# A hybrid decoder block on one core: the order of the first loads, dummy matmuls up to the first product, and a new order of the mixer's products

## The chip, the cores and the metric

The kernel runs on one core of a Trainium2 chip. TensorE (PE) multiplies, VectorE (DVE) and ScalarE (ACT) work element by element, GpSimd (POOL) and SyncE (SP) mostly issue transfers here. The metric is the device time of one execution in microseconds (us). Lower is better.

## The reference

One layer of a decoder trunk over 16 meta tokens and 256 tokens, width 2048, in float32:

```python
u = rms_norm(h, g_pre_mix[l])
proj = u @ w_in[l]
z_pool, v_conv, g_conv, gate_a, gate_b = jnp.split(proj, splits, axis=-1)
y_a = causal_multiscale_pool(z_pool, w_pool_grp[l], pool_scale[l]) @ w_pool_out[l]
y_b = conformer_conv(v_conv, g_conv, w_dw[l], b_dw[l],
                     conv_ln_g[l], conv_ln_b[l]) @ w_conv_out[l]
m = jax.nn.sigmoid(gate_a) * y_a + jax.nn.sigmoid(gate_b) * y_b
h = h + rms_norm(m @ w_o[l], g_post_mix[l])
u = rms_norm(h, g_pre_mlp[l])
f = jnp.square(jax.nn.relu(u @ w_up[l])) @ w_down[l]
h = h + rms_norm(f, g_post_mlp[l])
```

The convolution has 31 taps per channel and is followed by a LayerNorm and a swish. The output is the 256 tokens without the meta tokens.

## The kernel before

**Numbers.** Every float32 operand is split in a rounded high part (a copy on ACT, `hi`) and the rest (a subtraction on DVE, `lo`), and a product is three matmuls: high by high, high by low, low by high. The weights come in blocks of 1 MB (128 partitions by 2048 floats), each loaded by a DMA that SP issues, split by one ACT copy and one DVE subtraction, and read by PE. Three split blocks are held at a time.

**Start.** SP and ACT issue the first loads: the meta tokens, the gain row `g_pre_mix`, the tokens `x` in four blocks of 512 columns (the first in two halves of 128 tokens, `load_x` and the lines around it), and the first two weight chunks in small pieces (`open_chunk`, L335). POOL issues five rows of vectors and the taps (`load_rows`, L396, L425). PE runs dummy transposes of an identity (`keep_warm`, L434), turns the gain row into a column (L403), then the meta tokens (`meta_tiles`, L482) and the token tiles (`x_tile`, L472). ACT and DVE scale and split them into `u` (L474, L475, L490, L491). Then a loop over the 16 row tiles k turns token tile k + 3, splits weight piece k + 3 (`pieces_to`) and multiplies tile k (`mm3`, L515).

**Mixer.** What follows is planned when the kernel is built. `Plan.add` takes work with an engine, a cost and names read and written; `Plan.order` simulates the engines: PE's order is fixed by the program, the others take the ready work with the earliest due time, and transfers share the DMA by `ISSUE` (issue and start-up time of a queue) and `LANDS`. The result fixes the instruction order of every engine; the real waits are semaphores. PE's order is the table `MAIN`, one word a step. First letter: p is the projection of the pooling branch, a and b are the two gates, c the convolution's projection, o the output projection. A word with two digits, such as a13, is two plain products (both halves of 128 tokens) of column block 1 and row block 3. A word with P, such as a0P5, is one of seven products that stand for eight (Strassen's scheme) on column blocks 0 and 1: P5, P6, P4 and P7 need the sum of two weight blocks. The sum is made on DVE where the table `SUMMED` names it (L805); elsewhere POOL issues a DMA that adds the second block onto the first while it lands (L809, "bring"). T31 turns column block 3 of the second token half of the merged branches for the output projection (L1303; low part L1312). `fu`, `OF` and `um8` make the combined activations ("forms") that the P-products read; `lnm` and `lnv` are the matmuls for the LayerNorm's mean and variance (L1042, L1072), after which half 0 and half 1 of its result (`s_act`, L1100) are made; `CD`, `h1`, `k0r`, `k1` open rooms. While PE multiplies, DVE also does the 240 taps of the convolution (L923).

**MLP.** A second plan of the same kind, from about 510 us to the end (L520, L526, L1921).

## Time and profile before

| | us |
|---|---|
| median of 3 runs | 1193.89 |
| lowest, highest | 1192.64, 1197.27 |
| the profiled execution | 1195.48 |
| its span | 1193.4 |

The profile is of one execution. Idle time of an engine is put down to what ended it. A row of the timeline is a start, a length in us, the engine, the line, the operation, the names written and read, and the count. Names lose their numbers in the profile, so bank_k is any of four PSUM banks and acc_v either of two.

### The profile page before, as it was taken

What the parts mean: (1) busy time and instruction counts of PE and PEld (TensorE: products, weight loads), DVE (VectorE), ACT (ScalarE), POOL (GpSimd) and SP (SyncE); (2) the same over time, 40 slices, a digit from 0 to 9 for tenths busy, and PEclk for the clock granted to TensorE, in tenths of its full rate; (3) what the DMA queues carried; (4) which work ended last, traced back from release to release, by engine and by line L of the source; (5) the groups of instructions that cost most, each with busy time, mean ns of one, the idle gap of its engine ahead of it and who ended that gap; (6) DMA issues with size and microseconds to landing.
All of it is one profiled execution on the core that took longest, in us unless ns stands there. A gap on an engine that the chain in (4) does not pass through costs nothing.

```text
span 1193.4 us, 15768 instructions
## 1 busy us (share of the span) xinstructions
PE 1171.5 (98%) x6318; PEld 1012.9 (85%) x6318; DVE 1079.1 (90%) x1162; ACT 711.5 (60%) x718; POOL 53.3 (4%) x54
## 2 busy tenths in 40 slices
PE   9999999999999999999999999999999999999996
PEld 8999988777878777898888888888888888888885
DVE  6799999999998988687989989989999999899856
ACT  7634354565478746557776666666656756666542
POOL 1000000000000000000100000000000000000000
PEclk9999999999999999999999999999999999999998
DMA  9756353878767779549998897998998998979931
GB/s 314 249 183 218 107 173 109 282 199 285 203 198 253 247 229 316 177 128 359 230 343 222 244 317 179 261 310 191 297 279 213 306 236 233 316 184 264 329 140 71
DMA packets 181481, 280.23 MB, mean 235 GB/s; under 512 B 4657, under 2 KB 92145, under 8 KB 180496
## 3 DMA queue, kind: packets, MB, share of 16 engines
q1 hardware_dynamic: 160224, 235.35, 58.1%
q0 software_dynamic: 20160, 42.10, 19.9%
q10 hardware_dynamic: 1024, 1.78, 0.4%
q8 instruction: 49, 0.80, 0.3%
q14 instruction: 24, 0.20, 0.0%
HBM read 275.02 MB, written 4.19 MB: 234 GB/s over the span
## 4 chain that ended last, share of the span: by engine, by line
PE 76%; DVE 14%; DMA 4%; issue 3%; ACT 2%; DVEq 0%; POOL 0%; ACTq 0%; POOLq 0%
PE bank_u L520 18%; PE acc_up L1921 13%; PE bank_u L526 9%; PE bank_a L1921 7%; PE bank_k L1199 7%; DVE lo L793 6%; PE bank_k L515 6%; PE bank_b L1921 5%; DMA raw_p<-in_w_in_dram 3%; PE acc_v L515 3%; DVE c L923 3%; PE acc_v L1199 3%; PE acc_up L520 1%; ACT hi L788 1%; DVE raw_p L805 1%
## 5 line engine op out<-in xcount | busy, mean ns | idle before, releaser
L520 PE MATMUL bank_u<-m,hi 128*128 128x512 f32 x960 | 329.4, 390 | 0.0
L526 PE MATMUL bank_u<-m,lo 128*128 128x256 f32 x960 | 265.3, 276 | 0.0
L520 PEld LDWEIGHTS bank_u<-m,hi 128*128 128x128 f32 x960 | 180.2, 188 | 37.8
L788 ACT CAST hi<-raw_p 128x2048 fp32r<-128x2048 f32 x70 | 134.1, 1915 | 114.5 <-PE bank_k L1199 34.3
L526 PEld LDWEIGHTS bank_u<-m,lo 128*128 128x128 f32 x960 | 180.2, 188 | 1.6
L1747 DVE TENSOR_TENSOR lo<-raw_m,hi 128x2048 fp32r<-128x2048 f32 x71 | 162.5, 2289 | 15.2 <-ACT hi L1742 14.9
L793 DVE TENSOR_TENSOR lo<-raw_p,hi 128x2048 fp32r<-128x2048 f32 x70 | 160.0, 2290 | 16.9 <-ACT hi L788 16.7
L1742 ACT CAST hi<-raw_m 128x2048 fp32r<-128x2048 f32 x71 | 136.0, 1916 | 51.4 <-PE bank_u L520 18.0
L1921 PE MATMUL acc_up<-hi,forms 128*128 128x512 f32 x440 | 143.0, 390 | 0.7 <-ACT G L1946 0.7
L1742 ACT CAST hi<-raw_h 128x2048 fp32r<-128x2048 f32 x46 | 88.1, 1915 | 50.2 <-PE bank_u L520 32.5
L1747 DVE TENSOR_TENSOR lo<-raw_h,hi 128x2048 fp32r<-128x2048 f32 x46 | 105.3, 2290 | 12.8 <-ACT hi L1742 12.7
L923 DVE SCALAR_TENSOR_TENSOR c<-a,taps,c 128x256 f32<-128x256 f32 x240 | 100.5, 485 | 0.0
L1921 PEld LDWEIGHTS acc_up<-hi,forms 128*128 128x128 f32 x440 | 82.6, 188 | 18.8 <-ACT G L1946 1.1
L515 PE MATMUL bank_k<-u_um,hi 128*128 128x272 f32 x512 | 95.2, 287 | 0.0
L1199 PE MATMUL bank_k<-hi,u_um 128*128 128x512 f32 x272 | 86.8, 391 | 1.8 <-DVE sg L1244 1.1
L1921 PE MATMUL acc_up<-lo,forms 128*128 128x512 f32 x220 | 85.9, 391 | 0.0
L1921 PE MATMUL bank_a<-hi,forms 128*128 128x512 f32 (+1 forms) x256 | 82.0, 383 | 0.0
L515 PEld LDWEIGHTS bank_k<-u_um,hi 128*128 128x128 f32 x512 | 79.7, 188 | 0.0
L515 PE MATMUL bank_k<-u_um,lo 128*128 128x272 f32 x256 | 73.3, 287 | 0.0
L1742 ACT CAST hi<-raw_a 128x2048 fp32r<-128x2048 f32 x23 | 44.0, 1914 | 34.0 <-PE bank_u L520 25.0
L1921 PE MATMUL bank_b<-hi,forms 128*128 128x512 f32 (+1 forms) x200 | 63.4, 381 | 0.0
L1747 DVE TENSOR_TENSOR lo<-raw_a,hi 128x2048 fp32r<-128x2048 f32 x23 | 52.7, 2291 | 11.3 <-ACT hi L1742 11.3
(392 smaller groups left out, 2248.1 us busy)
## 6 DMA issues: line engine op xcount, KB each, us to landing
raw_p<-in_w_in_dram SPq DMA_DIRECT2D x34, 1024.0 KB, 5.8
raw_m<-in_w_up_dram SPq DMA_DIRECT2D x25, 1024.0 KB, 9.8
raw_m<-in_w_down_dram SPq DMA_DIRECT2D x22, 1024.0 KB, 8.5
raw_h<-in_w_down_dram SPq DMA_DIRECT2D x21, 1024.0 KB, 7.6
raw_h<-in_w_up_dram SPq DMA_DIRECT2D x16, 1024.0 KB, 8.7
raw_a<-in_w_down_dram SPq DMA_DIRECT2D x12, 1024.0 KB, 5.6
raw_a<-in_w_up_dram SPq DMA_DIRECT2D x11, 1024.0 KB, 7.0
raw_m<-in_w_down_dram POOLq DMA_DIRECT2D x11, 1024.0 KB, 9.2
```

What stands on the lines that cost most here:

```text
L515: nc.tensor.matmul(acc, w[:, k[0], cs], act[:, k[1], a, off:], start=first and n == 0, stop=last and n == 2)
L520: nc.tensor.matmul(acc.rearrange("p (a t) -> p a t", a=2)[:, :, ts], hi[:, k[0], cs], act[:, k[1], :, off + ts.start:off + ts.stop], start ...
L526: nc.tensor.matmul(acc[:, :T], lo[:, k[0], cs], act[:, k[1], 0, off:], start=False, stop=stop, skip_group_check=True)
L788: nc.scalar.copy(box["flat"], rooms[q]())
L793: nc.vector.tensor_sub(lo, rooms[q](), f32(box["flat"]))
L805: plan.add("DVE", 2.22, lambda a=at_rooms[0], b=at_rooms[1]: nc.vector.tensor_add(rooms[a](), rooms[a](), rooms[b]()), reads=names, writes ...
L923: nc.vector.scalar_tensor_tensor(C_c()[:, q, :], A_a()[:, q, i:i + T], taps[:, q, i:i + 1], C_c()[:, q, :], op0=ALU.mult, op1=ALU.add)
L1199: nc.tensor.matmul(banks[bank], a_(k, part), box[w_][:, k, :], start=opens and k == 0 and i == 0, stop=ends_ and k == CK - 1 and i == 2, s ...
L1742: nc.scalar.copy(box["flat"], raw_in(room))
L1747: nc.vector.tensor_sub(lo, raw_in(room), f32(box["flat"]))
L1921: nc.tensor.matmul(acc, forms[h][:, f, k, a_, :], box[w_][:, k, cs], start=start and k == 0 and n == 0, stop=stop and k == KH - 1 and n == ...
```

## The change

1. The first loads are issued in another order: the two halves of token block 0 first (one on ACT's queue, one on SP's), then the meta tokens (SP) and the gain row (ACT), then the weight pieces with token blocks 1, 2 and 3 between them on SP (`X_BEHIND`). The five vector rows and the taps go from POOL's queue to SP's, behind the third weight chunk.
2. The meta tokens' split is cut in four parts: the first behind token tile 0, the others in the first three turns of the loop. The loop multiplies tile k before it turns tile k + 3.
3. Of 14 + 4 dummies, 13 stay ahead of the gain's transpose, and 5 stand between the third token tile and the first product.
4. The planner's constants change (`ISSUE`, `LANDS`, `SHARE`, costs of transfers): while both queues move data, POOL's gets 3.55 times the share of SP's.
5. `MAIN` is a new order of the same 96 steps, and `SUMMED` makes 9 instead of 11 sums on DVE: a0P5, a2P6, c2P5 and o0P5 become DMA additions, a2P7 and o0P4 become sums.

```diff
-DUMMIES = 4
+DUMMIES = (13, 5)
@@
 MAIN = (
-    "p00 p01 fu p11 p10 p20 p30 p21 p31 k1 a0P1 a0P5 a13 a0P6 a12 a0P7 a03 a0P3 a2P1 a0P4 a2P5 "
-    "a02 a33 a2P6 a2P3 a2P2 a2P7 a23 a32 a0P2 b0P1 a22 a2P4 b0P5 b32 b23 b33 b21 b22 lnm b0P6 b20 "
-    "b0P7 lnv b03 b12 b0P2 b13 b0P4 b0P3 k0r b30 b31 b02 um8 c01 c2P1 c2P5 c00 c2P6 c2P3 c2P7 "
-    "c2P2 c2P4 T00 T01 c10 CD T31 T30 o0P1 c11 T20 o23 T11 T10 o20 o21 T21 OF o22 o0P5 o0P6 o0P3 "
-    "o0P7 o12 o0P2 o03 o0P4 o13 h1 o02 o30 o31 o32 o33 ")
-SUMMED = {('gate0', 0): '567', ('gate0', 2): '56', ('gate1', 0): '5', ('co', 2): '564', ('o', 0): '56'}
+    "p00 p01 p30 p31 p21 p20 fu p10 p11 k1 a0P1 a0P2 a2P1 a0P5 a13 a12 a0P6 a0P3 a0P7 a02 a0P4 "
+    "a2P5 a2P2 a32 a03 a2P6 a2P3 a33 a2P7 a22 a23 a2P4 b33 b32 b20 b0P1 b31 b0P5 b23 b22 b0P6 "
+    "b0P3 lnm b0P7 b30 b21 lnv b12 b0P2 b0P4 b02 b13 b03 k0r um8 c2P1 c00 c11 c01 T00 c2P5 c2P6 "
+    "c2P3 c10 T01 c2P7 T10 o20 c2P2 T11 c2P4 o0P1 CD T30 T31 o21 T20 T21 o23 OF o0P2 o0P5 o22 o13 "
+    "o0P6 o0P3 o0P7 o12 o0P4 h1 o03 o02 o30 o31 o32 o33 ")
+SUMMED = {('gate0', 0): '67', ('gate0', 2): '57', ('gate1', 0): '5', ('co', 2): '46', ('o', 0): '46'}
@@ class Plan
-    ISSUE = {"SP": (0.4, 1.0), "POOL": (1.28, 2.2)}
-    LANDS = 1.0
+    ISSUE = {"SP": (0.4, 1.09), "POOL": (1.28, 2.44)}
+    LANDS = 1.13
+    SHARE = {"SP": 1.0, "POOL": 3.55}
@@ def open_chunk
             nc.sync.dma_start(raw[:, sl, :], src[:, sl, :])
+            if (n, b_) in X_BEHIND:
+                load_x(X_BEHIND[n, b_])
@@
-    nc.sync.dma_start(m_in, meta)
-    pre_rows = load_rows(nc.scalar, "g_pre_mix")
-    for t, queue in enumerate((nc.scalar, nc.sync)):
-        queue.dma_start(x_in[:, t, :CW], xv[:, t, :CW])
-    load_x(nc.scalar, 1)
-    for b in range(2, XB):
-        open_chunk()
-        load_x(nc.sync, b)
-    open_chunk()
-    other_rows = load_rows(nc.gpsimd, "pool_scale", "b_dw", "conv_ln_g", "conv_ln_b", "g_pre_mlp")
+    X_BEHIND = {(0, 4): 1, (0, 8): 2, (1, 4): 3}
+    for t, queue in enumerate((nc.scalar, nc.sync)):
+        queue.dma_start(x_in[:, t, :CW], xv[:, t, :CW])
+    nc.sync.dma_start(m_in, meta)
+    pre_rows = load_rows(nc.scalar, "g_pre_mix")
+    for _ in range(FIRST + 1):
+        open_chunk()
     taps_in = big.tile([TAPS, CC], F32, tag="c", name="taps_in")
-    nc.gpsimd.dma_start(taps_in, w_dw)
+    nc.sync.dma_start(taps_in, w_dw)
+    other_rows = load_rows(nc.sync, "pool_scale", "b_dw", "conv_ln_g", "conv_ln_b", "g_pre_mlp")
@@
-    keep_warm(14)
+    keep_warm(DUMMIES[0])
     rows_to_columns(*pre_rows)
-    keep_warm(DUMMIES)
@@
-    for k in range(-LEAD, KD):
-        if k + LEAD < KD:
-            x_tile(k + LEAD)
-        pieces_to(k + LEAD + 1)
-        if k < 0:
-            continue
+    def turn_and_split(k):
+        if k < KD:
+            x_tile(k)
+        if k == 0:
+            meta_parts.pop(0)()
+        pieces_to(k + 1)
+
+    for k in range(LEAD):
+        turn_and_split(k)
+    keep_warm(DUMMIES[1])
+    for k in range(KD):
+        for j, acc in enumerate(accs):
+            mm3(acc, *opened[k // HALF[0]][:2], u, (k % HALF[0], k), slice(j * P, (j + 1) * P),
+                k == 0, k == KD - 1)
+        turn_and_split(k + LEAD)
+        if k < 3:
+            meta_parts.pop(0)()
...
-        for j, acc in enumerate(accs):
-            mm3(acc, *opened[k // HALF[0]][:2], u, (k % HALF[0], k), slice(j * P, (j + 1) * P),
-                k == 0, k == KD - 1)
```

In the planner a moving transfer advances by its queue's share of the sum of shares instead of by an equal part, and its cost falls from 3.1 or 2.9 to 3.06 or 2.87 on SP, from 5.9 to 4.94 for an addition on POOL.

How PE's rows move at the start (idle is the dummies' bank, pv the gain's transpose, mt_in the meta tokens', xt a token tile's, acc_v the first product). Before:

```order
L434 MATMUL idle<-ident 128x128 x14
L403 MATMUL pv_g_pre_mix<-ident,rows_g_pre_mix 128x16
L434 MATMUL idle<-ident 128x128 x4
L482 MATMUL mt_in<-ident,m_in 128x16 x16
L472 MATMUL xt_185<-ident,x_in 128x128 x2
L472 MATMUL xt_192<-ident,x_in 128x128 x2
L472 MATMUL xt_199<-ident,x_in 128x128 x2
L472 MATMUL xt_206<-ident,x_in 128x128 x2
L515 MATMUL acc_v_0_183<-u_um,hi_83 128x272 x2
```

The same place in the change (its own line numbers):

```order
L436 MATMUL idle<-ident 128x128 x13
L407 MATMUL pv_g_pre_mix<-ident,rows_g_pre_mix 128x16
L483 MATMUL mt_in<-ident,m_in 128x16 x16
L473 MATMUL xt_172<-ident,x_in 128x128 x2
L473 MATMUL xt_181<-ident,x_in 128x128 x2
L473 MATMUL xt_188<-ident,x_in 128x128 x2
L436 MATMUL idle<-ident 128x128 x5
L519 MATMUL acc_v_0_170<-u_um,hi_83 128x272 x2
```

The four dummies behind the gain's transpose are gone, five stand ahead of the first product, and the fourth token tile comes behind it.

POOL's row of block additions in the mixer (w_in holds the gates; raw_p, raw_k, raw_um, raw_s0b are rooms). Before:

```order
L809 DMA raw_p_417<-in_w_in_dram 128x4x512
L809 DMA raw_p_415<-in_w_in_dram 128x4x512
L809 DMA raw_k_2237<-in_w_in_dram 128x4x512
L809 DMA raw_p_417<-in_w_in_dram 128x4x512
L809 DMA raw_p_415<-in_w_in_dram 128x4x512 x2
L809 DMA raw_p_416<-in_w_conv_out_dram 128x4x512
```

In the change:

```order
L822 DMA raw_p_415<-in_w_in_dram 128x4x512 x2
L822 DMA raw_p_417<-in_w_in_dram 128x4x512 x2
L822 DMA raw_p_416<-in_w_in_dram 128x4x512
L822 DMA raw_p_417<-in_w_in_dram 128x4x512 x2
L822 DMA raw_p_416<-in_w_conv_out_dram 128x4x512
L822 DMA raw_p_415<-in_w_conv_out_dram 128x4x512
```

Seven blocks of the gates and two of the convolution's projection are added by DMA, instead of six and one; two of the output projection stay.

DVE around T21, where m is the low part of a turned block, q_m and forms_o serve the output projection's P-products. Before:

```order
L805 TENSOR_TENSOR raw_p_416<-raw_p_416,raw_um_3358 128x2048
L1169 TENSOR_TENSOR sg_2259<-acc_v_0_183,sg_2259 128x512
L1312 TENSOR_TENSOR m<-bank_y_413,m 128x4x128
L1312 TENSOR_TENSOR m<-bank_y_414,m 128x4x128
L793 TENSOR_TENSOR lo_3740<-raw_p_415,hi_3702 128x2048
L1171 TENSOR_TENSOR sg_2259<-sg_2259,ya 128x512
L1113 TENSOR_TENSOR q_m<-q_m 128x512 x2
L1117 SCALAR_TENSOR_TENSOR q_m<-q_m 128x512
L793 TENSOR_TENSOR lo_3764<-raw_p_416,hi_3756 128x2048
L1115 TENSOR_TENSOR q_m<-q_m 128x512
L805 TENSOR_TENSOR raw_p_416<-raw_p_416,raw_p_417 128x2048
L1312 TENSOR_TENSOR m<-bank_y_414,m 128x4x128
```

In the change:

```order
L1184 TENSOR_TENSOR sg_2268<-sg_2268,ya 128x512
L1325 TENSOR_TENSOR m<-bank_y_414,m 128x4x128
L806 TENSOR_TENSOR lo_3741<-raw_p_416,hi_3713 128x2048
L1126 TENSOR_TENSOR q_m<-q_m 128x512
L806 TENSOR_TENSOR lo_3764<-raw_p_415,hi_3743 128x2048
L1126 TENSOR_TENSOR q_m<-q_m 128x512
L1325 TENSOR_TENSOR m<-bank_y_413,m 128x4x128
L1325 TENSOR_TENSOR m<-bank_y_414,m 128x4x128
L1140 TENSOR_TENSOR forms_o<-q_m,forms_o 128x4x128
L1130 SCALAR_TENSOR_TENSOR q_m<-q_m 128x512
L1140 TENSOR_TENSOR forms_o<-q_m,forms_o 128x4x128
```

Before, a sum of two blocks (L805) stands between the last split and the last m; in the change no sum stands there.

More of the change, by code (lines that the diff above doesn't have):

```diff
@@ L124, in next_landing @@
             if moving:
-                push(t + max(0.0, min(m[0] for m in moving.values())) * len(moving), "lands", stamp[0])
+                wait = min(m[0] / self.SHARE[q] for q, m in moving.items())
+                push(t + max(0.0, wait) * sum(map(self.SHARE.get, moving)), "lands", stamp[0])
         def release(i):
@@ L486, in meta_tiles, with part @@
         nc.vector.tensor_mul(mt, pt, vecs[:, g0:g0 + KD, None].broadcast_to([P, KD, M]))
-        for ks in (slice(0, K_FIRST), slice(K_FIRST, KD)):
-            for i, (hi, lo) in enumerate(zip(u.meta(ks, 0), u.meta(ks, 1))):
-                src = mt[:, ks.start:ks.stop - 1, :] if i == 0 else mt[:, ks.stop - 1, :]
-                nc.scalar.copy(hi, src)
-                nc.vector.tensor_sub(lo, src, f32(hi))
+        def part(ks, i):
+            hi, lo = u.meta(ks, 0)[i], u.meta(ks, 1)[i]
+            src = mt[:, ks.start:ks.stop - 1, :] if i == 0 else mt[:, ks.stop - 1, :]
+            nc.scalar.copy(hi, src)
+            nc.vector.tensor_sub(lo, src, f32(hi))
+        return [lambda ks=ks, i=i: part(ks, i)
+                for ks in (slice(0, K_FIRST), slice(K_FIRST, KD)) for i in range(2)]
     def sq_tile(b, t):
```

20 lines of the change are left out of this document (10 added, 10 removed).

## The prediction

> **What bounds the kernel now.** I read the page first, then busy time by stretch, then what TensorE (PE) waited for, then the first microseconds in order of time.
>
> ```profile
> span 1193.4 us, 15768 instructions
> PE 1171.5 (98%) x6318; PEld 1012.9 (85%) x6318; DVE 1079.1 (90%) x1162; ACT 711.5 (60%) x718; POOL 53.3 (4%) x54
> ```
>
> PE is busy 1171.5 of 1193.4 us. The change runs the same matmuls in another order, so only its 21.9 idle us, and stretches in which it runs slowly, can be won. The next view, stretches of the span (length, then busy us of each engine, granted clock, DMA share), tells where they lie.
>
> ```profile
> core 0: us, PE busy (x) PEld busy (x) DVE busy (x) ACT busy (x) POOL busy (x), PEclk, DMA share, GB/s
> 0.00:6.10 6.10, 4.74 (x22) 4.05 (x23) 0.17 (x1) 1.49 (x2) 4.22 (x14) 1.00 0.64 170
> 6.10:9.50 3.40, 2.52 (x25) 2.11 (x24) 1.88 (x8) 1.92 (x8) 0.00 (x0) 1.00 1.08 346
> 9.50:13.00 3.50, 3.50 (x16) 3.46 (x16) 2.99 (x8) 2.21 (x7) 0.00 (x0) 0.51 1.08 353
> 13.00:25.00 12.00, 12.00 (x101) 12.00 (x100) 9.27 (x23) 11.31 (x33) 0.00 (x0) 1.00 1.09 353
> ...
> 100.00:164.00 64.00, 63.60 (x517) 63.40 (x516) 63.95 (x109) 27.37 (x29) 0.00 (x0) 1.00 0.48 158
> 164.00:300.00 136.00, 133.16 (x580) 107.79 (x579) 132.54 (x159) 76.83 (x61) 6.48 (x5) 1.00 0.71 217
> 300.00:382.00 82.00, 81.12 (x359) 66.83 (x358) 77.44 (x85) 54.15 (x53) 1.27 (x1) 1.00 0.72 228
> 382.00:460.00 78.00, 74.37 (x337) 59.89 (x336) 72.39 (x62) 48.78 (x48) 5.14 (x5) 1.00 0.76 231
> ...
> 620.00:1180.00 560.00, 560.00 (x2897) 479.70 (x2896) 510.54 (x441) 344.95 (x301) 30.85 (x24) 1.00 0.86 245
> ```
>
> From 620 to 1180 us PE has no idle time: the MLP gives nothing. The products of the mixer lose 0.40 + 2.84 + 0.88 + 3.63 = 7.75 us between 100 and 460 us, and the start loses 1.36 + 0.88 us idle and about half of the 3.5 us at clock 0.51. From 100 to 164 us VectorE (DVE) is busy 63.95 of 64 us, and 132.54 of 136 after that: it splits each 1 MB weight block in two parts and does the 240 convolution taps, and is the engine that PE nearly waits for. What PE waited for:
>
> ```profile
> PE bank_k L1199 <- DVE lo L793: 1.7, 2, 1.0
> PE bank_k L1199 <- DVE m L1312: 1.5, 1, 1.5
> ...
> PE bank_k L1199 <- DVE sg L1244: 1.1, 2, 0.8
> PE acc_v L515 <- ACT hi L338: 0.9, 1, 0.9
> PE bank_y L1072 <- DVE sq L1065: 0.9, 1, 0.9
> ...
> PE bank_y L1303 <- DVE sg L1171: 0.7, 1, 0.7
> PE bank_k L1199 <- ACT sg L1248: 0.7, 1, 0.7
> PE bank_y L1303 <- DVE m L1312: 0.5, 1, 0.5
> ```
>
> Columns: total us, times, longest. L1199 is every mixer product, L793 a block's low part, L1072 the LayerNorm variance, L1303 the transposes of the merged branches and L1312 their low parts.
>
> **The start, part by part.** PE and then ScalarE (ACT), in order of time (start, length, engine, line),
>
> ```profile
> 1.36 3.25 PE L434 MATMUL idle<-ident 128*128 128x128 f32 x14 [1.36 <-POOL ident masks.py:199]
> 4.54 0.28 PE L403 MATMUL pv_g_pre_mix<-ident,rows_g_pre_mix 16*128 16x16 f32 x1
> 4.75 1.11 PE L434 MATMUL idle<-ident 128*128 128x128 f32 x4
> 5.79 1.29 PE L482 MATMUL mt_in<-ident,m_in 16*128 16x16 f32 x16
> 8.98 0.62 PE L515 MATMUL acc_v<-u_um,hi 128*128 128x272 f32 x2 [0.88 <-ACT hi L338]
> ...
> 12.18 0.43 PE L515 MATMUL acc_v<-u_um,lo 128*128 128x272 f32 x1
> ...
> 13.15 0.28 PE L515 MATMUL acc_v<-u_um,lo 128*128 128x272 f32 x1
> ```
>
> ```profile
> 7.58 0.69 ACT L490 CAST u_um<-mt 128x192 fp32r<-128x192 f32 x4 [3.93 <-DVE mt L486]
> ...
> 8.17 0.47 ACT L474 ACTIVATE u_um<-xt,vecs 128x256 fp32r<-128x256 f32 x1
> ...
> 8.54 0.39 ACT L338 CAST hi<-raw 128x256 fp32r<-128x256 f32 x1
> ```
>
> and three issues of transfers (count, KB, us from issue to landing):
>
> ```profile
> raw_s0a<-in_w_in_dram SPq DMA_DIRECT2D x2, 1024.0 KB, 13.1
> ...
> x_in<-in_x_dram ACTq DMA_DIRECT2D x1, 256.0 KB, 4.9
> ...
> rows_g_pre_mix<-in_g_pre_mix_dram ACTq DMA_DIRECT2D x1, 8.0 KB, 3.0
> ```
>
> The first product waits for a chain on ACT: four casts of the meta tokens, the first token tile, the first weight piece. The change leaves one of the four casts ahead of the tile; the casts take 8.17 - 7.58 = 0.59 us, so about 0.4 goes. It takes the four dummies between the gain's transpose and the meta transposes away: from 4.75 to 5.79, 1.0 us. Against that, the gain row g_pre_mix is issued second on ACT's queue, behind a 256 KB token block. From its issue at about 1.2 us it lands after 3.0 (its own row) to 4.9 us (the block's), so its transpose starts between 4.35 (when 13 dummies of 3.25 / 14 us end) and 5.7 instead of 4.54. I take 5.05, because the block's own issue moves from 1.19 to about 0.73 and its bytes are then the first that the engines move: +0.5. First product: 8.98 - 1.0 - 0.4 + 0.5 = 8.1, a gain of **0.9**, ends 0.25 and 1.5.
>
> The order of loads on SP puts weight rows 0 to 3 ahead of the second token block, which left ACT's queue; SP also takes six small loads from POOL, seven more issues in all, ahead of the two raw_s0a blocks. Those are the ones queued behind. They land 13.1 us (median) after issue at a DMA share of 1.08 to 1.09 in the stretches above, so bytes, not issues, set their landing, and the bytes are the same. I cost the move at nothing; cover is the 2.9 us of one further 1 MB block at 353 GB/s, and if it is gone ACT waits 1 to 2 us.
>
> **The clock.** These are the weight loads of the dummies and of the token transposes (minimum, median, maximum ns):
>
> ```profile
> L434 PEld LDWEIGHTS idle<-ident x18: 180/230/230, 1.4 to 5.2; 128*128 128x128 f32 x18
> ...
> L472 PEld LDWEIGHTS xt<-ident,x_in x32: 137/140/225, 7.0 to 22.4; 128*128 128x128 f32 x32
> ```
>
> The dummies run at the slow rate (230) until about 6.1, the token transposes from 7.0 at the fast one (140), and those of 9.5 to 13.0 slow again: the stretch behind the 0.88 us gap runs at half speed, and a 272-column matmul takes 0.43 there and 0.28 after it. With five dummies from the last of the three transposes to the first product the gap closes; if the stretch then runs at full speed, 0.49 of its 3.5 us, 1.7, is won. ACT limits that: it is idle 1.29 us from 9.5 to 13 and 0.69 from 13 to 25, 2.0 in all, and its work doesn't shrink. I take **1.5**, ends 0 and 1.7. [...]
>
> **The mixer's products.** One product (12 matmuls) takes 2.72 us; an N-step is two of them.
>
> ```profile
> 499.02 2.72 PE acc_v L1199 x12
> ```
>
> ```profile
> L805 DVE TENSOR_TENSOR raw_p<-raw_p,raw_p x5: 2283/2293/2301, 202.4 to 449.9; 128x2048 f32<-128x2048 f32 x5
> ```
>
> ```profile
> DMA to landing us min/median/max: 8.5/9.2/12.5
> ```
>
> ```profile
> L1072 PE MATMUL bank_y<-sq,ones x2: 379/431/483, 339.4 to 339.8; 128*128 128x256 f32 x2
> ...
> L1100 DVE TENSOR_TENSOR s_act<-c,s_act x2: 1219/1220/1221, 363.5 to 375.0; 128x1024 fp32r<-128x1024 f32 x2
> ```
>
> The row of landings (minimum, median, maximum us) is that of the blocks that POOL adds by DMA. The same 96 steps run in another order, so I go by places.
>
> *Merged branches.* Before, o22 follows the transpose T21 at once and needs what it writes (the 1.5), and T31, T30 and their readers follow their inputs closely (0.7 + 0.5). Now T20 and T21 are followed by o23, o0P2 and o0P5 (5.4 + 2.7 + 2.7 = 10.9 us) before o22, and T30, T31 by o21 (5.4). All **2.7** goes; ends 1.2 (the forms for o0P5, late by the same 1.5) and 2.7.
>
> *LayerNorm.* Between mean and variance stood b0P6, b20, b0P7 (10.9 us) and PE waited 0.9. Now b0P7, b30, b21: 13.6. **0.9** goes. Behind the variance stood 42 us of products, now 28 to c2P1, which reads half 0, and 36 to c11, which reads half 1. Those halves were ready at 363.5 + 1.2 and 375.0 + 1.2, that is 25.3 and 36.8 us after the variance. So half 0 has 2.7 us to spare and half 1 is 0.8 late: **-0.8**, ends 0 and -2.5 (one more 2.3 us split ahead of it).
>
> *Gates.* Two sums of 2.29 us leave DVE for POOL (a0P5, a2P6, c2P5 and o0P5 are now added by DMA, a2P7 and o0P4 no longer), and the LayerNorm, by which the taps must be done, moves back from 158 to 169 us of products. DVE, 97% busy from 164 to 300 (132.54 of 136), loses 2 to 4% of that and gets the 11 us. The lo wait there (1.0 of the 1.7) and both sg waits (1.1 + 0.7) come to 2.8; I take two thirds, **1.9**, ends -8.5 (below) and 2.8. Of the lo wait in the c steps (0.7) I take **0.3**, ends -0.7 and 0.7. The waits not listed stay. The planner's other constants are costed only through the order they give; in the MLP it swaps neighbours on DVE and ACT, where PE never waits, at nothing, and without that cover a swap costs one 2.3 us split.
>
> Sum: 0.9 + 1.5 + 2.7 + 0.9 - 0.8 + 1.9 + 0.3 = **7.4 us**. The profiled execution took 1195.48 (span 1193.4 and 2.1 around it), which gives 1188.1; it lies 1.6 above the median of the three runs, 1193.89, which I forecast against: **1186.5**.
>
> **Rivals.** *DVE keeps the pace.* It is full from 100 to 164 us; if it is the bound up to 300, PE's earlier start and the gates' term are swallowed. For it: 63.95 of 64. Against it: PE idles only 0.4 there, and DVE's work is released by PE's products, so it should move along. Gain 7.4 - 2.4 - 1.9 = 3.1: 1190.8.
>
> *The dummies don't hold the clock* (that the change doesn't do what it says): transposes fill an engine thinly, and the stretch that went slow was 2.52 us busy of 3.40. Against it: the 1.5 us wait on L1312 lies between 382 and 460 us, where the clock stayed at 1.00. Then 7.4 - 1.5 = 5.9: 1188.0. [...]
>
> *A block added by DMA comes late (slower).* a0P5 reads the room of a0P1, which must be split first; then 9.2 to 12.5 us of transfer, a cast (1.9) and a low part (2.3): 13.4 to 16.7 us, with a0P2, a2P1 and a0P1 itself (8.2 us of products) as cover. A summed block took 2.3 instead. For it: the wait for a block is in no other way so long. Against: splits run up to three products ahead, which adds up to 8 us of cover. Without that head start PE waits up to 16.7 - 8.2 = 8.5, the gates' 1.9 is not won, and the result is 5.5 - 8.5 = 3.0 us slower, 1196.9. It decides from a wait of 5.5 us on.
>
> **How the numbers follow.** Forecast 0.64, DVE 0.16, clock 0.13, late block 0.07. About 0.5%, 6.0 us, is what a measurement of this kernel can tell from no change, so faster means under 1187.9. Of the forecast some 0.54 lies there and of the clock's case half, 0.06: faster **0.60**. Slower (over 1199.9) needs the late block at two places: **0.05**; the same: **0.35**. The forecast's own range is 1184 to 1189.5; all upper ends (1.5 + 1.7 + 2.7 + 0.9 + 0 + 2.8 + 0.7 = 10.3) reach 1183.6, and the DVE case with half 1 late by 2.5 is 1192.5. I give **1183.0 to 1193.5**.
>
> **What would show it.** Right: the first product near 8.1 us, the clock 1.00 from 9.5 to 13, no wait of L1303 or of the products behind T21 over 0.3, none at the variance, a short wait at c11, PE idle in the mixer near 3 us. Wrong: a wait for DMA or ACT before a0P5, DVE full with PE idle between 200 and 300, the start gained and lost again by 160 us, or a row of dummies with the clock still at half behind it.

## The result, and the profile after

| | us |
|---|---|
| before, median of 20 runs (lowest, highest) | 1194.77 (1192.64, 1198.71) |
| changed, median of 20 runs (lowest, highest) | 1191.91 (1190.44, 1193.56) |
| ratio of changed to before, 95% interval | 0.9975 [0.9967, 0.9983] |
| span of the profiled execution, before and changed | 1193.4, 1190.3 |

The change gains 2.9 us, a quarter of a per cent; 7.4 were forecast. The time lies inside the range given, but near its slow end, and the gain isn't the forecast one made smaller: a larger gain and two losses stand behind it. The head of the page of the changed kernel, then the same stretches of the span as in the prediction, then PE's waits:

```profile
span 1190.3 us, 15769 instructions
PE 1168.5 (98%) x6318; PEld 1014.1 (85%) x6318; DVE 1075.7 (90%) x1160; ACT 708.8 (60%) x718; POOL 52.6 (4%) x50
```

```profile
0.00:6.10 6.10, 3.04 (x13) 2.63 (x13) 0.00 (x0) 1.49 (x2) 0.88 (x8) 1.00 0.69 148
6.10:9.50 3.40, 2.06 (x18) 2.02 (x19) 0.20 (x2) 0.00 (x0) 0.00 (x0) 1.00 1.07 328
...
100.00:164.00 64.00, 64.00 (x521) 63.88 (x519) 63.94 (x109) 28.00 (x28) 0.00 (x0) 1.00 0.45 149
164.00:300.00 136.00, 133.45 (x591) 109.66 (x591) 132.70 (x170) 75.24 (x63) 5.28 (x4) 1.00 0.76 233
300.00:382.00 82.00, 82.00 (x363) 67.96 (x362) 74.78 (x76) 55.61 (x52) 5.14 (x4) 1.00 0.78 219
382.00:460.00 78.00, 78.00 (x360) 64.42 (x360) 75.58 (x64) 51.37 (x53) 4.59 (x4) 1.00 0.91 282
...
560.00:620.00 60.00, 56.96 (x283) 47.82 (x282) 53.98 (x42) 40.66 (x37) 4.85 (x4) 1.00 0.97 267
620.00:1180.00 560.00, 558.54 (x2896) 478.50 (x2894) 511.33 (x446) 341.81 (x303) 30.86 (x24) 1.00 0.84 243
```

```profile
PE pv_g_pre_mix L407 <- DMA rows_g_pre_mix<-in_g_pre_mix_dram: 3.0, 1, 3.0
PE acc_v L1212 <- ACT sg L1261: 1.9, 1, 1.9
PE bank_b L1934 <- DVE lo L1760: 1.6, 1, 1.6
PE acc_up L1934 <- ACT G L1959: 1.4, 1, 1.4
...
PE bank_u L524 <- DVE F_raw L1839: 0.5, 1, 0.5
...
PE bank_k L1212 <- DVE lo L806: 0.3, 1, 0.3
```

Three things are to be seen. At the start PE is busy 3.04 + 2.06 us up to 9.5 instead of 4.74 + 2.52, and its longest wait is for the gain row. From 300 to 460 us it has no idle time left (4.51 us before). In the MLP, where PE had 0.69 us idle from its first product to the last row (665.01 of 665.70 busy), stand three waits of 3.5 us together (the rows of L1934 and L524).

Where the time went is read from a few instructions that both kernels have, in order: the second chunk's first product, the first product of the table (p00), the MLP's first, and the last matmul on a low part but for the tail. In the kernel before and then in the changed one, by their start:

```profile
25.54 0.41 PE L515 MATMUL bank_k<-u_um,hi 128*128 128x272 f32 x2
...
164.14 0.40 PE L1199 MATMUL bank_k<-hi,y 128*128 128x512 f32 x1
...
516.04 0.62 PE L520 MATMUL acc_up<-m,hi 128*128 128x256 f32 x3
...
1181.74 0.28 PE L1921 MATMUL bank_b<-lo,forms 128*128 128x256 f32 x1
```

```profile
27.40 0.41 PE L519 MATMUL bank_k<-u_um,hi 128*128 128x272 f32 x2
...
166.02 0.40 PE L1212 MATMUL bank_k<-hi,y 128*128 128x512 f32 x1
...
509.54 0.62 PE L524 MATMUL acc_up<-m,hi 128*128 128x256 f32 x3
...
1178.64 0.28 PE L1934 MATMUL bank_b<-lo,forms 128*128 128x256 f32 x1
```

Up to the first p product the change loses 1.9 us, measured against this one execution of the kernel before; three other kernels below keep its start, and reach that product at 162.0 to 163.4, so the loss may be up to 4.0. From there to the MLP ("the mixer's stretch") it takes 343.5 instead of 351.9: 8.4 won. From the MLP's first product to the last row ("the MLP's stretch") 669.1 instead of 665.7: 3.4 lost. 8.4 - 1.9 - 3.4 = 3.1, the difference of the two spans.

The same instructions in every kernel that was run, in us; the ratio is to the kernel before, run beside each:

| kernel | first product | second chunk | first p | MLP's first | last row | mixer's stretch | MLP's stretch | ratio, 95% interval |
|---|---|---|---|---|---|---|---|---|
| before | 8.98 | 25.54 | 164.14 | 516.04 | 1181.74 | 351.9 | 665.7 | 1 |
| changed | 11.62 | 27.40 | 166.02 | 509.54 | 1178.64 | 343.5 | 669.1 | 0.9975 [0.9967, 0.9983] |
| row_first | 10.62 | 27.02 | 165.63 | 508.88 | 1181.29 | 343.3 | 672.4 | 0.9957 [0.9944, 0.9971] |
| meta_and_row_first | 8.51 | 24.24 | 166.78 | 509.73 | 1179.12 | 343.0 | 669.4 | 0.9979 [0.9967, 0.9991] |
| start_mended | 7.66 | 24.44 | 163.07 | 506.05 | 1175.43 | 343.0 | 669.4 | 0.9947 [0.9934, 0.9959] |
| small_loads_on_POOL | 11.85 | 28.32 | 166.94 | 509.54 | 1180.47 | 342.6 | 670.9 | 0.9969 [0.9958, 0.9980] |
| no_dummies | 7.68 | 24.76 | 163.38 | 507.68 | 1179.66 | 344.3 | 672.0 | 0.9954 [0.9938, 0.9969] |
| mlp_old_constants | 11.00 | 27.47 | 166.08 | 508.75 | 1175.21 | 342.7 | 666.5 | 0.9937 [0.9925, 0.9950] |
| both_mended | 7.13 | 22.64 | 167.16 | 510.17 | 1177.32 | 343.0 | 667.2 | 0.9943 [0.9931, 0.9956] |
| table_alone | 8.15 | 23.53 | 162.16 | 509.33 | 1175.04 | 347.2 | 665.7 | 0.9953 [0.9937, 0.9969] |
| constants_alone | 8.50 | 24.78 | 163.41 | 514.51 | 1184.14 | 351.1 | 669.6 | 1.0022 [1.0010, 1.0033] |
| all_mended | 8.50 | 23.98 | 162.60 | 505.07 | 1170.76 | 342.5 | 665.7 | 0.9915 [0.9901, 0.9928] |
| start_undone | 8.39 | 23.41 | 162.02 | 504.75 | 1171.39 | 342.7 | 666.6 | 0.9928 [0.9914, 0.9943] |
| a2P1_later | 8.50 | 24.38 | 163.01 | 506.54 | 1172.23 | 343.5 | 665.7 | 0.9933 [0.9920, 0.9946] |

### The profile page after: what moved, and what is told of

It reads as the page before. It is cut to its first block, busy times and chain, and to the rows that moved or that the text cites. A ratio compares the mean times of both kernels' runs of the same rounds, so it can differ in the third digit from the quotient of the medians.

```text
span 1190.3 us, 15769 instructions
## 1 busy us (share of the span) xinstructions
PE 1168.5 (98%) x6318; PEld 1014.1 (85%) x6318; DVE 1075.7 (90%) x1160; ACT 708.8 (60%) x718; POOL 52.6 (4%) x50
## 4 chain that ended last, share of the span: by engine, by line
PE 82%; DVE 11%; DMA 4%; issue 2%; ACT 1%; DVEq 0%; ACTq 0%
PE bank_u L524 18%; PE acc_up L1934 12%; PE bank_k L1212 12%; PE bank_u L530 9%; PE bank_a L1934 7%; PE acc_v L1212 7%; PE bank_b L1934 5%; PE bank_k L519 5%; DVE lo L806 5%; DVE c L936 4%; PE acc_v L519 3%; DMA raw_k<-in_w_in_dram 2%; PE acc_up L524 1%; PE acc_v L1472 1%; PE bank_u L1934 1%
## 5 line engine op out<-in xcount | busy, mean ns | idle before, releaser
L524 PE MATMUL bank_u<-m,hi 128*128 128x512 f32 x960 | 329.6, 390 | 0.5 <-DVE F_raw L1839 0.5
L524 PEld LDWEIGHTS bank_u<-m,hi 128*128 128x128 f32 x960 | 180.3, 188 | 38.7 <-DVE F_raw L1839 0.8
L1934 PE MATMUL acc_up<-hi,forms 128*128 128x512 f32 x440 | 143.2, 390 | 1.4 <-ACT G L1959 1.4
L1934 PEld LDWEIGHTS acc_up<-hi,forms 128*128 128x128 f32 x440 | 82.7, 188 | 19.4 <-ACT G L1959 1.8
L1934 PE MATMUL acc_up<-lo,forms 128*128 128x512 f32 x220 | 86.0, 391 | 0.0
L1934 PE MATMUL bank_a<-hi,forms 128*128 128x512 f32 (+1 forms) x256 | 82.1, 384 | 0.0
L1934 PE MATMUL bank_b<-hi,forms 128*128 128x512 f32 (+1 forms) x200 | 63.5, 381 | 0.0
L1212 PEld LDWEIGHTS bank_k<-hi,u_um 128*128 128x128 f32 x280 | 52.6, 188 | 10.9
```

The lines of the kernel that those rows point to most:

```text
L524: nc.tensor.matmul(acc.rearrange("p (a t) -> p a t", a=2)[:, :, ts], hi[:, k[0], cs], act[:, k[1], :, off + ts.start:off + ts.stop], start ...
L1212: nc.tensor.matmul(banks[bank], a_(k, part), box[w_][:, k, :], start=opens and k == 0 and i == 0, stop=ends_ and k == CK - 1 and i == 2, s ...
L1934: nc.tensor.matmul(acc, forms[h][:, f, k, a_, :], box[w_][:, k, cs], start=start and k == 0 and n == 0, stop=stop and k == KH - 1 and n == ...
```

## The experiments

### The start

The first microseconds of the changed kernel, PE, ACT's queue and SP's queue in turn:

```profile
1.36 3.04 PE L436 MATMUL idle<-ident 128*128 128x128 f32 x13 [1.36 <-POOL ident masks.py:199]
7.44 0.28 PE L407 MATMUL pv_g_pre_mix<-ident,rows_g_pre_mix 16*128 16x16 f32 x1 [3.05 <-DMA rows_g_pre_mix<-in_g_pre_mix_dram]
7.57 1.86 PE L483 MATMUL mt_in<-ident,m_in 16*128 16x16 f32 x16
...
12.22 0.43 PE L519 MATMUL acc_v<-u_um,lo 128*128 128x272 f32 x1
```

```profile
1.18 0.45 ACTq L400 DMA_DIRECT2D rows_g_pre_mix<-in_g_pre_mix_dram  x1
```

```profile
11.23 1.58 SPq L426 DMA_DIRECT2D taps_in<-in_w_dw_dram  x1
...
16.96 4.82 SPq L780 DMA_DIRECT2D raw_s0a<-in_w_in_dram  x2
```

The gain row is issued at 1.18 and lands at 7.4, 6.2 us later instead of 3.0. PE stands idle for 3.05 us and then works at the slow rate (0.43 for a 272-column matmul, 0.28 to 0.29 when fast). The clock column of the stretches above nevertheless reads 1.00 from 6.1 to 13, as it does for the slow dummies of the first 6.1 us: the trace holds no record of the clock before 12.94 us (before 6.13 in the kernel before), so up to there that column says nothing, and the rate has to be read from the length of the matmuls. The raw_s0a blocks, behind taps and vector rows now, are issued at 16.96; before it was

```profile
11.31 5.54 SPq L767 DMA_DIRECT2D raw_s0a<-in_w_in_dram  x2
```

**row_first.** The row goes ahead of the token half block on ACT's queue:

```diff
+    pre_rows = load_rows(nc.scalar, "g_pre_mix")
     for t, queue in enumerate((nc.scalar, nc.sync)):
         queue.dma_start(x_in[:, t, :CW], xv[:, t, :CW])
     nc.sync.dma_start(m_in, meta)
-    pre_rows = load_rows(nc.scalar, "g_pre_mix")
```

> The changed kernel with the gain row issued ahead of the token half block on ACT's queue; meta tokens still behind their half block on SP's. Theory (what lies ahead in the same queue delays a small load): the row lands about 3.0 us after its issue as before, its transpose starts at 4.4 when the 13 dummies end; but the 128 KB of meta tokens now show the same delay, landing near 7.4 as the row did, so the first product stays at 11.0 to 11.6 us and the whole time within 0.6 us of the changed kernel's (ratio to the kernel before 0.9970 to 0.9975). Rival (only the row was late, the meta tokens land by 5): meta transposes from 4.7, first product 8.0 to 9.0, the time 1.9 to 2.6 us under the changed kernel's (0.9953 to 0.9959).

```profile
4.49 0.28 PE L407 MATMUL pv_g_pre_mix<-ident,rows_g_pre_mix 16*128 16x16 f32 x1
6.54 1.89 PE L483 MATMUL mt_in<-ident,m_in 16*128 16x16 f32 x16 [1.76 <-DMA m_in<-in_meta_dram]
```

The row's wait is gone at once, and the wait for the meta tokens, which still stand behind 256 KB, takes its place: they are issued at 1.19 and used at 6.54, 5.4 us later (2.9 from issue to landing in the kernel before). The first product comes at 10.62, the theory's side, a little under its 11.0, and the first p product only 0.4 us before the changed kernel's. The same two small loads take 2.5 us (the meta tokens, 5.4 to their use against 2.9) and 3.2 us (the row, 6.2 in the changed kernel against 3.0) longer behind a token half block on their own queue than ahead of it in the kernel before. The ratio, 0.9957, is the rival's, though its interval touches the changed kernel's; the 0.4 us of the profile don't explain that, and the run is inconclusive on the whole time (the profile is of the slowest of its five executions, 1194.75, with a half-clock stretch in the MLP).

**meta_and_row_first.** Both small loads ahead, as in the kernel before (the line for `m_in` moves too).

> The changed kernel with the meta tokens and the gain row issued ahead of the two token half blocks, as in the kernel before; everything else of the change stays. Theory: row and meta land by 4.4, the token halves near 6.1 as before, the first product starts at 8.0 to 8.6 us, the products of the second chunk (27.40 in the changed kernel, 25.54 before) start at 24.7 to 25.5, and the time falls by 1.9 to 2.7 us against the changed kernel (ratio to before 0.9952 to 0.9959). Rival (the weight bytes or ACT set the end of the first loop, whenever it starts): the first product is early but the second chunk's products still start at 27 or later and the time moves by less than 0.7 us.

The first product starts at 8.51 and the second chunk 3.2 us earlier, and the first p product still 0.8 us *later* than in the changed kernel. PE's waits that lie between, ACT's cast of the block that it waits for, and PE by the microsecond (the number before the last two is the clock):

```profile
31.42 0.52 PE L519 MATMUL bank_k<-u_um,hi 128*128 128x272 f32 x2 [0.29 <-ACT hi L801]
33.74 0.59 PE L519 MATMUL bank_k<-u_um,lo 128*128 128x272 f32 x1 [1.81 <-DVE lo L806]
```

```profile
29.46 1.90 ACT L801 CAST hi<-raw_s0a 128x2048 fp32r<-128x2048 f32 x1 [4.36 <-DMA raw_s0a<-in_w_in_dram]
```

```profile
33.00:34.00 1.00, 0.26 (x1) 0.26 (x2) 0.69 (x1) 1.00 (x1) 0.00 (x0) 0.80 1.09 343
34.00:35.00 1.00, 1.00 (x5) 1.00 (x6) 0.62 (x1) 0.97 (x4) 0.00 (x0) 0.50 1.10 351
```

The block lands at 29.46, as in the changed kernel (29.47), and sets the time whenever PE begins; the rival was right about that. What it left out is the price behind the wait: 2.1 us idle, then 3.4 us at half clock (33.6 to 37.0). Of seven executions one kept a mean clock of 0.997 and took 1190.2 us; the other six had 0.992 to 0.996 and took 1192.6 to 1194.3.

**start_mended.** The small loads return to POOL's queue as well:

```diff
-    nc.sync.dma_start(taps_in, w_dw)
-    other_rows = load_rows(nc.sync, "pool_scale", ...)
+    nc.gpsimd.dma_start(taps_in, w_dw)
+    other_rows = load_rows(nc.gpsimd, "pool_scale", ...)
```

> The changed kernel with meta tokens and gain row issued first, and the five vector rows and the taps back on POOL's queue; table, sums and constants as changed. Theory (the small loads that the change puts ahead of the raw_s0a blocks on SP's queue delay these: they were issued at 17.0 and landed near 29.4 with the engines nearly empty at 26 to 28 us, against 11.3 and under 25.9 before): the first raw_s0a block lands by 26, the waits of 0.3 and 1.8 us behind 31 us and the half clock after them are gone, the second chunk's products start at 24.2 (22.6 if the clock rises early as in one of the two runs) and the first p product at 162.8 (161.2), 3.2 to 4.8 us before the changed kernel's 166.0; the time is 3.0 to 4.8 us under the changed kernel (ratio 0.9935 to 0.9950). Rival one (the bytes of the weights set it): the waits behind 31 us stay in some form and the first p product starts after 165. Rival two (DVE, full from 50 to 164 us, keeps the pace): no wait before 50 us, but PE waits for DVE between 50 and 164 and the first p product again starts after 165.

```profile
11.41 5.82 SPq L780 DMA_DIRECT2D raw_s0a<-in_w_in_dram  x2
```

```profile
25.22 1.91 ACT L801 CAST hi<-raw_s0a 128x2048 fp32r<-128x2048 f32 x1
```

The block is issued at 11.4 and cast at 25.2 with no wait for it. The first p product starts at 163.07, 2.95 us before the changed kernel's: just short of the theory's 3.2, and its ratio is in the theory's range. The first rival falls, and so does the second: DVE is as full between 100 and 164 us as ever (63.95 of 64).

Which of the small loads does the harm was not tried by a run, but the trace's records of single transfers point at the taps. On SP's queue their 31 rows of 4 KB move strictly one after another, from 18.9 to 25.3 us in the changed kernel; on POOL's queue in the kernel before, all 31 start within 1.0 us (8.2 to 9.2).

**small_loads_on_POOL.** The fourth corner: only these loads return, row and meta tokens stay late.

> The changed kernel with only the five vector rows and the taps back on POOL's queue; the gain row and the meta tokens stay behind the token half blocks. It is the fourth corner of a square: row late or early, small loads on SP or on POOL. Theory (the late first product covers the late raw_s0a blocks, so each of the two faults hides the other): the raw_s0a blocks land by 26 again, but the first product stays at 11 to 12 us, the second chunk's products at 27.0 to 27.6 and the first p product at 165.6 to 166.4; the time within 1 us of the changed kernel's (ratio 0.9965 to 0.9983). Rival (the small loads alone cost the start, by delaying the weight pieces): the second chunk's products at 25.5 or earlier, the first p product before 164.5, and 1.5 us or more under the changed kernel.

The first p product starts at 166.94, no earlier than in the changed kernel (0.5 us beyond the range, and the second chunk 0.7 beyond its own, with the clock at half until about 14.6), and the ratio stays at 0.9969. So each fault hides the other. With the first product late, the late blocks cost nothing; with the blocks late, an early first product is worth nothing. Only both repairs together win the 3 us.

**no_dummies.** start_mended with `DUMMIES = (13, 0)`.

> The kernel of the run start_mended without the five dummies between the token transposes and the first product (13 and 0 instead of 13 and 5). Theory (the dummies close the gap and so keep or bring the clock): a gap of about 1 us stands ahead of the first product again, and the granted clock or the rate of the first products (a 272-column matmul 0.43 instead of 0.28 or 0.29 us) is slow for 3.4 us behind it or until later than with the dummies; the second chunk's products start 1 to 1.7 us later than in start_mended. Rival (the gap doesn't matter to the clock, ACT paces the loop): the second chunk's products start within 0.4 us of start_mended's, or earlier by up to 0.4.

The gap is there (0.67 us ahead of the first product), but the second chunk starts only 0.3 us later than in start_mended, the rival's outcome. start_mended itself, with the dummies and no gap ahead of the first product, ran fast up to 7.6 and then at half clock until 11.0. all_mended, with the same start, had no such fall, but there the fast rate came only at 9.1. start_mended's stretches, then two rows of all_mended (the same 16 meta transposes took 1.14 in start_mended):

```profile
6.10:9.50 3.40, 3.26 (x18) 2.98 (x19) 2.40 (x7) 2.36 (x7) 0.00 (x0) 0.72 1.05 323
9.50:13.00 3.50, 3.50 (x25) 3.50 (x24) 2.00 (x8) 2.31 (x8) 0.00 (x0) 0.78 1.08 368
```

```profile
4.45 1.86 PE L483 MATMUL mt_in<-ident,m_in 16*128 16x16 f32 x16
...
9.10 0.30 PE L519 MATMUL acc_v<-u_um,lo 128*128 128x272 f32 x1
```

Of the five profiles with early row and meta tokens and with the dummies, only both_mended is fast from the meta transposes on without a fall. What the dummies are worth is therefore not settled by one profile of each; the 0.3 us is less than the spread between two executions of one start (24.44 and 23.98).

### The MLP

**mlp_old_constants.** The planner's old constants in the second plan alone; its order on ACT and DVE is then that of the kernel before, and SP's and POOL's never differed.

```diff
     plan = Plan()
+    plan.ISSUE = {"SP": (0.4, 1.0), "POOL": (1.28, 2.2)}
+    plan.LANDS = 1.0
+    plan.SHARE = {"SP": 1.0, "POOL": 1.0}
...
-        plan.add("SP", 3.06 if r[0][0] == "U" else 2.87, ...
+        plan.add("SP", 3.1 if r[0][0] == "U" else 2.9, ...
...
-                plan.add("POOL", 4.94, ...
+                plan.add("POOL", 5.9, ...
```

> The changed kernel with the planner's old constants in the MLP's plan alone; ACT's and DVE's order there is then the same as in the kernel before, SP's and POOL's are the same in all three. Theory (the constants' new order costs the MLP 3.4 us): the waits at 576.2 (1.6 us) and 583.2 (1.4 us) go, the stretch from the MLP's first product to the last returns from 669.1 to about 665.7, and the time falls by 2.7 to 3.8 us against the changed kernel (ratio 0.9943 to 0.9952). Rival (the MLP loses because it starts 6.5 us earlier and its first blocks come later relative to it, whatever the order): waits of about 3 us stay between 560 and 620, and the time stays within 1 us of the changed kernel's.

The MLP's stretch falls to 666.5 and the ratio to 0.9937: 0.0038 below the changed kernel's, some 4.5 us (3.2 by the medians; the theory had 2.7 to 3.8). In the profile stand 2.6 us in the MLP and 0.8 in the mixer's stretch, whose order is the same; the first product came 0.6 us earlier, the first p product no earlier. The wait of 1.6 us is gone, the one on G (1.4) stays in this run and is 0.7 in others. What the swap did is seen on DVE, in the kernel before and then in the changed one, with the wait that it leads to:

```profile
576.99 2.29 DVE L1747 TENSOR_TENSOR lo<-raw_c,hi 128x2048 fp32r<-128x2048 f32 x1
579.20 2.29 DVE L1747 TENSOR_TENSOR lo<-raw_m,hi 128x2048 fp32r<-128x2048 f32 x1
```

```profile
571.09 2.29 DVE L1760 TENSOR_TENSOR lo<-raw_m,hi 128x2048 fp32r<-128x2048 f32 x1
...
573.89 2.29 DVE L1760 TENSOR_TENSOR lo<-raw_c,hi 128x2048 fp32r<-128x2048 f32 x1 [0.18 <-ACT hi L1755]
```

```profile
576.24 0.50 PE L1934 MATMUL bank_b<-lo,forms 128*128 128x512 f32 x1 [1.64 <-DVE lo L1760]
```

The low part of raw_c, which PE needs first, now comes behind that of raw_m. In three other kernels with the new order (row_first, small_loads_on_POOL, no_dummies) that wait is longer, and the granted clock falls to 0.50 at it for 3.4 to 6.8 us; their MLP's stretches are the longest, 670.9 to 672.4. In row_first:

```profile
577.83 0.80 PE L1934 MATMUL bank_b<-lo,forms 128*128 128x512 f32 x1 [2.30 <-DVE lo L1760]
```

So the new order costs from 3.4 us, as in the changed kernel's profile, to 6.7. Over all kernels the new order's MLP takes 669.1 to 672.4 us and the old order's 665.7 to 667.2, whenever the MLP starts (504.8 to 516.0): the rival, which blamed the earlier start, falls.

**both_mended.** meta_and_row_first and mlp_old_constants together.

> The changed kernel with meta tokens and gain row issued first and the old constants in the MLP's plan: both suspected losses taken back. Theory (the losses are independent and both real): 4.6 to 6.4 us under the changed kernel, about 8.4 us under the kernel before (ratio 0.9920 to 0.9937). Rival (one of the two stays or an earlier start is swallowed by DVE before 164 us): under 3.8 us, ratio 0.9943 or more.

The rival's side by a hair (0.9943): the MLP gives its part (667.2), the start nothing, since the raw_s0a blocks were not yet mended. The expectation had not foreseen the waits behind 31 us.

**all_mended.** start_mended and mlp_old_constants together.

> The kernel of the run start_mended with the planner's old constants in the MLP's plan. Theory: both gains add: the first p product as in start_mended, the MLP's stretch (first product to last matmul) 666.5 to 667.2 us instead of 669.1; 5.5 to 7.5 us under the changed kernel (ratio to the kernel before 0.9913 to 0.9930). Rival (a start that is earlier moves the MLP's first blocks against its transfers and brings new waits there): the MLP's stretch is 669 or more and the time no better than start_mended.

0.9915, median 1185.28: 10.2 us under the kernel before beside it and the fastest of all; the MLP's stretch is that of the kernel before. PE's list of waits holds 1.5, 0.7 and 0.4 us and the 1.4 for the identity at the very start.

**start_undone.** all_mended with the start of the kernel before; all behind the first p product is in the same order.

> The kernel before with the new MAIN and SUMMED and the new planner's constants in the mixer's plan; old start, old constants in the MLP's plan. From the first p product on, the order on every engine is that of the run all_mended. Theory (the start's part of the change is worth nothing here even when mended, because the clock's phase in the first 13 us moves the start by about 1 to 2 us either way): the first p product at 162.2 to 164.1, the mixer's stretch 342.5 to 343.5, the MLP's 665.5 to 666.5, the whole within 1.5 us of all_mended (ratio 0.9908 to 0.9928). Rival (the mended start, with the meta split cut up and five dummies, gains its 0.9 + 1.5 us): 1.5 to 3 us above all_mended (ratio 0.9928 to 0.9940).

0.9928 is the border between the two. The profile has the first p product 0.6 us earlier than all_mended, the medians (1187.0 and 1185.3) speak for all_mended by 1.7, and the intervals overlap. Whether a mended new start is worth anything over the old one stays open. The clock's phase, by which the theory moves the start, was my estimate; measured is only the spread of one start, 23.41 to 25.54 us to the second chunk in the four kernels with the old one.

### The mixer

**table_alone.** The kernel before with the new `MAIN` and `SUMMED` and nothing else.

> The kernel before with the new MAIN and SUMMED alone: the old start, the old constants in both plans. Theory (the table and the sums make the mixer's gain, the constants little of it): from the first p product to the MLP's first 343 to 345 us instead of 351.9, the MLP's stretch 665.5 to 666.5, the whole 7 to 9 us under the kernel before (ratio 0.9925 to 0.9941). Rival (the new table needs the constants that it was found with: DVE's and POOL's order come out otherwise): the mixer's stretch is 347 us or more.

```profile
164.00:300.00 136.00, 131.46 (x577) 107.74 (x576) 135.64 (x177) 74.11 (x59) 5.20 (x4) 1.00 0.77 235
...
382.00:460.00 78.00, 78.00 (x360) 64.36 (x359) 75.57 (x65) 51.40 (x53) 5.16 (x5) 1.00 0.94 293
```

The mixer's stretch is 347.2: the table and the sums make 4.7 of the 8.4 us, and the constants, which I had costed only through the order, the other 3.7. The rival was right. The merged branches' waits (382 to 460) go with the table; between 164 and 300 PE idles 4.5 us with the old constants and 2.6 with the new.

**constants_alone.** The kernel before with the new constants in both plans, old table and sums.

> The kernel before with the new planner's constants in both plans, old table and sums, old start. Theory (the constants win in the mixer and lose in the MLP by themselves, as the difference between the runs table_alone and start_mended suggests): the mixer's stretch 348 to 350 instead of 351.9, the MLP's 669 to 672 instead of 665.7, the whole from 2 us faster to 4 us slower than before (ratio 0.998 to 1.0035). Rival (the constants only fit the table that they were found with): the mixer's stretch is 351.5 or more and the whole 3 to 7 us slower (1.0025 to 1.006).

The mixer gains 0.8, the MLP loses 3.9, the whole is 0.2% slower. That lies in the theory's range for the whole, but its mixer of 348 to 350 was not reached: the constants help little without the table.

**a2P1_later.** `a0P1 a0P2 a0P5 a2P1 a13` on all_mended.

> The kernel of the run all_mended with a2P1 one product later in MAIN (a0P1 a0P2 a0P5 a2P1 a13 instead of a0P1 a0P2 a2P1 a0P5 a13). Theory (the one long wait left in the mixer, 1.5 to 1.9 us ahead of a2P1, is that for its block, which is loaded into a room that opens late and so lands 1.1 us after ACT is free for it; 2.7 us of product in front cover it): the wait falls under 0.6 us, the mixer's stretch to 341.0 to 341.6, the whole 0.9 to 1.5 us under all_mended. Rival (DVE, busy 134.5 of 136 us there, sets the pace, so the wait moves to the next product): waits of 1 to 2.5 us stay between 215 and 300, and the mixer's stretch is 342.3 or more.

```profile
213.93 0.50 PE L1212 MATMUL acc_v<-lo,forms_u 128*128 128x512 f32 x1 [1.55 <-DVE lo L806]
```

ACT's row for the block that a0P5 reads:

```profile
209.64 3.72 ACT L801 CAST hi<-raw_p 128x2048 fp32r<-128x2048 f32 x2 [2.29 <-DMA raw_p<-in_w_in_dram]
```

A wait as long as the old one now stands inside a0P5, and the mixer's stretch grows by 1.1: the rival's numbers, but for a wait that comes at 213.9 instead of behind 215. Its cause, DVE's pace, isn't what the trace shows. The block that a0P5 reads is added by POOL's DMA, issued at 200.9 and landed 8.7 us later; ACT stood idle 2.29 us for it, and DVE's split (211.6) and PE followed at once. The theory had the place wrong: counted in the order of `MAIN`, the wait of 1.5 us in all_mended (1.9 in the changed kernel) stands ahead of a13, the second word behind a2P1. There, by the profile, PE waits for copies out of accumulators (L1261) that ACT does behind its cast of raw_k, and that cast had waited 0.8 us for its transfer (1.1 in the changed kernel).

## Why the prediction failed, step by step

**The landing of the gain row** is the step that failed first: "I take 5.05 ... +0.5". It landed at 7.4, and at 6.8 and 7.7 in the two other kernels with that order. I had bounded it by the block's 4.9 us after issue, as if a transfer behind a block landed no later than a block. From the row's issue at 1.2 even that gives 6.1, not the 5.7 that I wrote. The block itself landed at about 6.0 (5.3 us after its issue at 0.73); what the row's 1.4 us beyond that consist of wasn't tried. In place of 0.9 us won to the first product stand 2.6 lost (against the profiled execution of before), of which the loop gave back 0.8; the shown cause is the row's and the meta tokens' place in their queues (row_first, meta_and_row_first).

**The move of the loads on SP**, "I cost the move at nothing", is the second. The seven issues ahead of the raw_s0a blocks delayed their issue by 5.65 us and their landing to 29.5. The cover that I named, bytes, was wrong: the engines were nearly empty at 26 to 27 us.

```profile
26.00:27.00 1.00, 1.00 (x8) 0.86 (x7) 1.00 (x3) 1.00 (x3) 0.00 (x0) 1.00 0.13 33
```

In the changed kernel it indeed cost nothing, but only because the first product was late: had the first step come true, 2.1 us of waits and the half clock behind them would have taken its gain (meta_and_row_first). Between 26 and 27 us only one transfer was in flight for more than half of the time, just behind the taps' 31 rows, which moved one at a time until 25.3. That a part of the first block stood behind these rows is my inference; no run moved the taps alone.

**The clock**, 1.5, was not won in the changed kernel: its products were still slow at 12.2 (0.43), although the sign that I had named, 1.00 in the clock column from 9.5 to 13, is there. The term rested on one execution's slow stretch: of the kernels with the old start, before and constants_alone have such a stretch in their profiles and table_alone and start_undone don't. Of those with the mended start, start_mended has it, with no gap ahead of the first product, so closing the gap was not enough; all_mended and a2P1_later don't, but their rate became fast only at 9.1 and 10.1.

**The MLP**, "at nothing", is the third failed step, 3.4 us. That PE never waits there was true of one order only. The price beside it, one 2.3 us split for a swap without cover, was about right for the swap shown (1.64 of it stood as idle time, 2.30 in three other kernels); there was more than one, and the half clock that followed such a wait in those three (3.4 to 6.8 us at 0.50) was not priced at all.

**The mixer** went as told, and further. The waits behind T21 and T31 (2.7) and at the variance (0.9) are gone, c11 doesn't wait (I had -0.8), the c steps' low part is on time (0.7, I had 0.3); the gates won 0.6 of idle time instead of 1.9. That sums to 4.9 us of listed idle time, near the 5.0 forecast. The stretch shrank by 8.4, because a listed wait is not its whole cost:

```profile
264.25 0.39 PE L1199 MATMUL bank_k<-hi,u_um 128*128 128x512 f32 x1
265.64 0.50 PE L1199 MATMUL bank_k<-lo,u_um 128*128 128x512 f32 x1 [1.00 <-DVE lo L793]
```

From start to start 1.39 us pass where a 512-column matmul takes 0.227 (2.72 / 12): 1.16 lost, 1.00 listed. Counted in the trace from each of the 1476 512-column matmuls between 160 and 518 us to the matmul behind it, the starts lie 12.1 us too far apart before and 4.7 after, a difference of 7.4, where the idle time listed between them differs by 4.7 (6.8 and 2.1); the rest of the 8.4 lies at other shapes or is not accounted for.

**The rivals.** DVE doesn't keep the pace: it was full again from 100 to 164 us (63.94 of 64) and PE had no idle time. In the changed kernel the dummies had no clock to hold, because the row was late; with the row on time they didn't hold it in start_mended and did in both_mended, so that rival stays open. That transposes fill PE thinly, its reason, was not shown: the 0.88 us idle from 6.1 to 9.5 in the kernel before are all the gap ahead of the first product. The block that comes late didn't: a0P5 ran without a wait, and the 1.9 us stand ahead of a13 for another reason. With the new constants it was late only in a2P1_later, with 2.7 us less of cover, by 1.55.

## What to carry to other kernels

A small load that everything waits for belongs ahead of the large ones on its own queue (here the gain row landed 6.2 us after its issue behind a token half block, 3.0 ahead of it), and small loads that nobody waits for can do harm ahead of large ones too (here on SP's queue, where the raw_s0a block was cast at 29.5 us, not on POOL's, 25.2); cost each transfer by what stands before it in its queue, not by a landing time from another place. When two faults can cover each other, mend them together before judging either. A planner's constants are part of every plan that uses them: fit them for one stage and the next one's order changes, so give each its own or look at each stage's waits.

## What the runs showed of the hardware

In these runs a short wait of PE cost its own length, or that and up to 6.8 us at half clock besides. Single waits of 1.86 us (changed, ahead of 222.5), 1.88 (start_mended, 219.5) and 2.34 (table_alone, 220.2) left the clock at 1.00. Single waits of 1.91 and 1.99 us, in no_dummies and constants_alone, were each followed by 3.4 us at 0.50 (220.1 to 223.5 and 261.0 to 264.4):

```profile
219.88 0.59 PE L1212 MATMUL acc_v<-hi,u_um 128*128 128x512 f32 x1 [1.91 <-ACT sg L1261]
```

```profile
260.22 0.50 PE L1201 MATMUL bank_k<-lo,forms_u 128*128 128x512 f32 x1 [1.99 <-DVE lo L795]
```

In both_mended 1.3 and 1.8 us with half a microsecond of work between them brought it to 0.50 from 31.65 to 38.5, 6.8 us; in meta_and_row_first 0.3 and 1.8 us with half a microsecond between cost 3.4 us at half clock. So the length of a wait alone doesn't decide it, and whether a second wait close by adds to it isn't shown. The slow stretch from 9.55 to 12.96 in the kernel before is 3.41 us long, that of start_mended (7.61 to 11.02) too, and 6.8 is twice that. What sets these lengths, and in which execution such a stretch falls, isn't shown.

Transposes alone brought the fast rate early: in both_mended the 16 meta transposes took 1.13 us from 4.41 on, in all_mended 1.86 from 4.45 on, with the same instructions ahead. In the four profiles of the old start the fast rate came between 4.1 and 6.1 us.
